# Hybrid decoder trunk, branch D: the triangular inverse's matmuls issued in turn over array positions, in one burst a step

## The chip, the cores and the metric

The kernel runs on one core of a Trainium2 chip. The metric is the device time of one execution in microseconds (us); the median of the runs shown counts. A profiled execution gives the trace; its rows are written as engine, line of the kernel, operation and tile. PE is TensorE, PEld its weight loads, DVE is VectorE, ACT is ScalarE, POOL is GpSimd and SP is SyncE, whose queue issues the transfers.

## The reference

One post-norm decoder layer over 256 tokens of width 1024: one wide input projection, five parallel branches with six heads of 64 (four heads of 96 in the last), gates, merging and a layer norm. The change touches branch D, a gated delta rule in chunks of 64 tokens:

```python
M = jnp.where(strict, jnp.einsum('bhnid,bhnjd->bhnij', kb, k) * decay, 0.0)
T = lax.linalg.triangular_solve(M + eye, ..., left_side=True, lower=True)
u = T @ (v * beta[..., None])
w = T @ (kb * jnp.exp(gc)[..., None])
...
def step(state, inp):
    v_new = u_i - w_i @ state
    o = qd_i @ state + qk_i @ v_new
    state = state * gl_i[..., None, None] + jnp.swapaxes(kd_i, -1, -2) @ v_new
```

So the inverse of a lower triangular matrix with ones on its diagonal is wanted for every head and chunk, and then a substitution over the chunks. The kernel sets up the whole 256-token triangle per head as two halves of 128 rows, inverts the diagonal blocks of 64, and substitutes block by block.

## The kernel before

**Units and ticks.** The weights stream in as units of up to 128x1024. For each unit the SP queue issues a load into one of seven `raw` buffers (L176), ScalarE makes the rounded high part `hi` (L123), VectorE the rest `lo` (L124), and TensorE multiplies in three passes, high by high, high by low, low by high (`mm3`, L128). A unit of a projection has three chunks, of 9, 9 and 6 matmuls; the chunk is followed by one tick. At each tick `stepper` advances up to three of the side streams by one `yield` each: the branches' own work is written as generators in the order base, c, levels, solve, b, a, gate_d, cross, norm. A plain `yield` makes a stream wait for the next tick, `yield 2` for the one after it. The program order of every engine comes from this interleaving; a planner in the framework then lays out each engine's queue, using its own model of the times, and may move an instruction ahead of others whose operands it takes to be late. Each engine works off its queue in order.

**Branch D.** The stream `base` (`d_base`) writes the 16x16 diagonal blocks of AT through a scratch in DRAM, inverts all of them on VectorE (L532, L534), writes the inverses to a second scratch (L542), and loads them with sixteen transfers (L550) into two tiles: Tc, the inverses, and Uc, their transposes. `levels` (`d_levels`) combines blocks of 16 to 32 and blocks of 32 to 64. Each such step is a product of a lower-left block with an inverse (`y`, L565 and L589), an evacuation to SBUF (L568, L593), a second product (`z`, L574 and L598; for the smaller size also its transpose `zt`, L576) and an evacuation on VectorE (L580, L582, L601). There are twelve blocks (six heads, two halves), and each position of 32 or 64 rows of the array handles twelve products in a row before the next position begins, with a tick in between. `solve` (`d_solve`) runs two generators of three heads side by side, each with matmuls (L617, L626, L632) and evacuations (L619, L628, L634) in turn. The PSUM tiles of all these steps come from a pool `tp` with two buffers. What follows is the output product (L648 to L651), a norm, the gate of branch D, and `mem_norm`, which waits for the flag `od` and makes the normalized memory that the last projections multiply.

An fp32 matmul of the program appears in the trace as two matmul records.

Of the kernel before, what the change touches and what calls it, by code (L numbers as in the profile page):

```python
# [12 lines left out]
ALU = mybir.AluOpType  # L13
AX = mybir.AxisListType

P = 128
# [4 lines left out]
H = 6  # L21
HD = 64
# [26 lines left out]
C_ID, C_TRI, C_ONE, C_LO, C_MA, C_MG1, C_MG2, C_MG3 = (  # L49
    0, 128, 256, 384, 385, 769, 1153, 1537)  # L50
# [25 lines left out]
def kernel(ctx: ExitStack, tc: tile.TileContext, T: dict, out: bass.AP):  # L76
# [7 lines left out]
    dr = ctx.enter_context(tc.tile_pool(name="dr", bufs=1, space=bass.MemoryType.DRAM))  # L84

    V_, A_, PE, G_ = nc.vector, nc.scalar, nc.tensor, nc.gpsimd
    uid = [0]

    def nm(s):
# [25 lines left out]
    def tpps(shape):  # L115
        return pst("tp", shape, 2)
# [6 lines left out]
        A_.activation(hi, src, AF.Copy)  # L123
        V_.tensor_tensor(lo, src, hi.bitcast(F32), op=ALU.subtract)  # L124

    def mm3(pt, lh, ll, rh, rl, first, last, keep=False):
        for l, r, start, stop in ((lh, rh, first, False), (lh, rl, False, False), (ll, rh, False, last)):
            ins = PE.matmul(pt, l, r, start=start, stop=stop)  # L128
            if keep:
                tc.keep_in_program_order(ins)  # L130

    def together(*products):
# [17 lines left out]
    def K(o, n=P):  # L150
        return cst[:, o:o + n]
# [96 lines left out]
    def stepper(gens, n, force=False):  # L248


        k = 0
        for g in list(gens):
            if k == n:
                break
            if not force and ready.get(id(g), 0) > tick[0]:
                continue
            try:
                d = next(g)
                if d is not False:
                    k += 1  # L260
                    ready[id(g)] = tick[0] + (GAP if d is None else d)
            except StopIteration:
                gens.remove(g)
# [244 lines left out]
    def d_base():  # L508

        yield from wait("AT")  # L510
        AT = R["AT"]
        ascr = dr.tile([8, 12, 16, 16], F32, name="ascr")
        t16, u16 = ct("t16", (96, 16, 16)), ct("u16", (96, 16, 16))
        a16, tmp = ct("a16", (96, 16, 16)), ct("tmp16", (96, 225))

        Tc, Uc = R["Tc"], R["Uc"] = spt("pr", (P, 12, 32), bufs=NPR), f3t(shape=(P, 12, 64))
        G_.memset(Tc, 0.0)
        G_.memset(Uc, 0.0)
        for b in range(8):
            r = slice(16 * b, 16 * b + 16)  # L520
            nc.sync.dma_start(ascr[b].rearrange("g j c -> j g c"), AT[r, 0:12, r])
            if b % 2:
                yield
        V_.memset(t16, 0.0)
        V_.memset(t16.rearrange("p i c -> p (i c)")[:, 0::17], 1.0)
        yield
        nc.sync.dma_start(a16, ascr.rearrange("b g j c -> (b g) j c"))
        for _ in range(4):
            yield
        for i in range(1, 16):  # L530
            pr = tmp[:, :i * i].rearrange("p (c j) -> p c j", c=i)
            V_.tensor_tensor(pr, t16[:, 0:i, 0:i].rearrange("p j c -> p c j"),  # L532
                             a16[:, 0:i, i][:, None, :].to_broadcast([96, i, i]), op=ALU.mult)
            V_.tensor_reduce(t16[:, i, 0:i], pr, axis=AX.X, op=ALU.add, negate=True)  # L534
            if i % 2 or i > 8:
                yield
        V_.tensor_copy(u16, t16.rearrange("p i c -> p c i"))
        yield
        scrs = []
        for src in (t16, u16):  # L540
            scr = dr.tile([8, 12, 16, 16], F32, name=nm("scr"))
            nc.sync.dma_start(scr.rearrange("b g j c -> (b g) j c"), src)  # L542
            scrs.append(scr)
        for _ in range(3):
            yield
        for b in range(8):
            r = slice(16 * b, 16 * b + 16)
            for scr, dst, n in zip(scrs, (Tc, Uc), (2, 4)):
                c = slice(16 * (b % n), 16 * (b % n) + 16)
                nc.sync.dma_start(dst[r, :, c], scr[b].rearrange("g j c -> j g c"))  # L550
            yield
        for _ in range(3):
            yield
        flag("base")

    def d_levels():

        yield from wait("base")
        AT, Tc, Uc = R["AT"], R["Tc"], R["Uc"]

        y = tpps((P, 12, 16))
        for b in range(4):
            r = slice(32 * b, 32 * b + 32)
            for g in range(12):
                PE.matmul(y[r, g], AT[r, g, r], Tc[r, g, 0:16], start=True, stop=True)  # L565
            yield
        ys = spt("Y", (P, 12, 32), bufs=1)
        A_.activation(ys[:, :, 0:16], y, AF.Copy)  # L568
        yield
        z, zt = tpps((P, 12, 16)), tpps((P, 12, 16))  # L570
        for b in range(4):
            r, c = slice(32 * b, 32 * b + 32), 32 * (b % 2)
            for g in range(12):
                PE.matmul(z[32 * b:32 * b + 16, g], ys[r, g, 0:16], Uc[r, g, c + 16:c + 32], start=True, stop=True)  # L574
                if b % 2 == 0:
                    PE.matmul(zt[r, g], Uc[r, g, 0:32], ys[r, g, 0:16], start=True, stop=True)  # L576
            yield
        for b in range(4):
            r, c = slice(32 * b, 32 * b + 32), 32 * (b % 2)
            V_.tensor_scalar(Uc[32 * b:32 * b + 16, :, c + 16:c + 32], z[32 * b:32 * b + 16], -1.0, None, op0=ALU.mult)  # L580
            if b % 2 == 0:
                V_.scalar_tensor_tensor(Tc[r, :, 0:16], zt[r], K(C_LO, 1)[r], Tc[r, :, 0:16], op0=ALU.mult, op1=ALU.add)  # L582
            yield

        ab = [(slice(64 * b, 64 * b + 32), slice(64 * b + 32, 64 * b + 64)) for b in range(2)]
        y = tpps((P, 12, 32))
        for i, j in ab:
            for g in range(12):
                PE.matmul(y[j, g], AT[i, g, j], Tc[i, g], start=True, stop=True)  # L589
            yield  # L590
        ys = spt("Y", (P, 12, 32), bufs=1)
        for i, j in ab:
            A_.activation(ys[j], y[j], AF.Copy)  # L593
        yield
        z = tpps((P, 12, 32))
        for i, j in ab:
            for g in range(12):
                PE.matmul(z[i, g], ys[j, g], Uc[j, g, 32:64], start=True, stop=True)  # L598
            yield
        for i, j in ab:  # L600
            V_.tensor_scalar(Uc[i, :, 32:64], z[i], -1.0, None, op0=ALU.mult)  # L601
        yield
        flag("levels")

    def d_solve():

        yield from wait("levels")
        AT, PT, Uc, V = R["AT"], R["PT"], R["Uc"], R["V"]
        W = f3t(shape=(P, 2, 6, HD))

        def solve(g):
            hs, hsl = range(3 * g, 3 * g + 3), slice(3 * g, 3 * g + 3)
            for t in range(2):
                if t == 1:
                    pt = tpps((P, 3, HD))
                    for x, h in enumerate(hs):
                        PE.matmul(pt[:, x], AT[:, 12 + h], W[:, 0, h], start=True, stop=True)  # L617
                    yield
                    V_.tensor_tensor(V[:, 1, hsl], V[:, 1, hsl], pt, op=ALU.subtract)  # L619
                    yield  # L620
                for b in range(2):
                    r = slice(64 * b, 64 * b + 64)
                    if b == 1:
                        pt = tpps((P, 3, HD))
                        for x, h in enumerate(hs):
                            PE.matmul(pt[r, x], AT[0:64, 6 * t + h, r], W[0:64, t, h], start=True, stop=True)  # L626
                        yield
                        V_.tensor_tensor(V[r, t, hsl], V[r, t, hsl], pt[r], op=ALU.subtract)  # L628
                        yield
                    pt = tpps((P, 3, HD))  # L630
                    for x, h in enumerate(hs):
                        PE.matmul(pt[r, x], Uc[r, 6 * t + h], V[r, t, h], start=True, stop=True)  # L632
                    yield
                    V_.tensor_copy(W[r, t, hsl], pt[r])  # L634
                    yield

        live = [solve(0), solve(1)]
        while live:
            stepper(live, 2)
            yield 1  # L640
        od = R["od"] = f3t(shape=(P, 2, 6, HD))
        rq = R["rq"]
        lg = lgps()[:, :, :384].rearrange("p t (h d) -> p t h d", h=6)
        for t in range(2):
            pt = lg[:, t]
# [335 lines left out]
    fin = {}  # L981
# [15 lines left out]
    def out_units():  # L997
# [3 lines left out]
        def out_mm(u, k, t, i, first, last):  # L1001
            lo, hi = PC[t][i]
            ts = slice(t * P, (t + 1) * P)
            yh, yl = (y[:, k % 3, ts] for y in yhl[k // 3])
            if k > 5:
                h, l = (x[lo // 512][:, lo % 512:lo % 512 + hi - lo] for x in (u.h, u.l))
            else:
                h, l = u.h[:, lo:hi], u.l[:, lo:hi]
            mm3(fin["p"][t][i][:, :hi - lo], yh, yl, h, l, first, last, keep=not first)

        def chunk(u, k, t):
            if k == 0 and t == 0:
# [169 lines left out]
```

## Time and profile before

| what | us |
|---|---|
| runs | 488.65, 488.16, 487.26; median 488.16 |
| the profiled execution | 489.4 |
| its span, first to last instruction | 487.6 |
| TensorE busy | 469.8, 96% of the span |
| VectorE busy | 336.1, 69% |
| ScalarE busy | 270.6, 55% |
| mean granted clock of TensorE | 0.977 of full speed |

Busy time of TensorE is the union of the modelled spans of its matmuls, which overlap; a busy TensorE is not one at its peak. The difference between the profiled execution's time and its span, 1.8 us, lies before the first and after the last instruction.

### The profile page before, as it was taken

How to read it: one execution, taken by the hardware profiler on the slowest of the kernel's cores; microseconds unless marked ns; L12 is line 12 of the kernel's file. 1: busy time of each engine (PE TensorE's matmuls, PEld its weight loads, DVE VectorE, ACT ScalarE, POOL GpSimd, SP SyncE). 2: the span in 40 equal slices, each digit the busy share in tenths (PEclk: the TensorE clock that was granted, in tenths of full speed). 3: DMA queues.
4: the chain of work that ended last, by engine and by line, in shares of the span. 5: the costliest groups of instructions: out<-in, count | busy, mean ns of one | idle time of the engine just before them, and what ended most of it. 6: DMA issues, size and time to landing. Idle time of an engine off the chain costs nothing.

```text
span 487.6 us, 10147 instructions
## 1 busy us (share of the span) xinstructions
PE 469.8 (96%) x3957; PEld 439.2 (90%) x3957; DVE 336.1 (69%) x764; ACT 270.6 (55%) x521; POOL 30.5 (6%) x36
## 2 busy tenths in 40 slices
PE   7999999989989999999999999999999999999994
PEld 3999999979988999999999999988987899999973
DVE  4898998875983435568976665666667457678747
ACT  5546684763773333466854455846657445566610
POOL 0000040120000000000001210000012111100000
PEclk9999999989998699999999999999999999999997
DMA  8995667554444113245656786252753345577302
GB/s 263 367 369 169 202 202 250 161 144 121 146 105 116 44 60 114 84 140 174 204 155 209 222 260 215 78 167 77 279 191 120 104 125 173 182 231 235 131 1 86
DMA packets 35050, 81.38 MB, mean 167 GB/s; under 512 B 8969, under 2 KB 17467, under 8 KB 34875
## 3 DMA queue, kind: packets, MB, share of 16 engines
q1 hardware_dynamic: 34715, 80.22, 52.1%
q8 instruction: 31, 0.51, 0.4%
q10 hardware_dynamic: 288, 0.52, 0.3%
q14 instruction: 16, 0.13, 0.1%
HBM read 79.37 MB, written 1.36 MB: 166 GB/s over the span
## 4 chain that ended last, share of the span: by engine, by line
PE 84%; DVE 6%; DMA 4%; ACT 3%; issue 1%; SPq 1%; POOL 0%; DVEq 0%; POOLq 0%
PE mm L128 67%; PE lg L135 3%; PE lg L128 2%; DVE lo L124 2%; PE tp L128 2%; ACT pr L754 2%; PE av L135 2%; PE lg L897 1%; PE lg L773 1%; DMA raw<-in_wcs_dram 1%; ACT hi L123 1%; DVE pr L738 1%; DMA scr<-t 1%; PE av L920 1%; PE tp L632 1%
## 5 line engine op out<-in xcount | busy, mean ns | idle before, releaser
L124 DVE TENSOR_TENSOR lo<-raw,hi 128x1024 fp32r<-128x1024 f32 (+4 forms) x163 | 170.7, 1049 | 89.6 <-ACT hi L123 89.0
L128 PE MATMUL mm<-xhi,hi 128*128 128x256 f32 x776 | 221.3, 285 | 0.4 <-ACT hi L123 0.4
L123 ACT ACTIVATE hi<-raw 128x1024 fp32r<-128x1024 f32 (+4 forms) x163 | 146.4, 901 | 131.8 <-PE mm L128 90.2
L128 PE MATMUL mm<-xhi,lo 128*128 128x256 f32 x776 | 219.2, 283 | 0.3 <-DVE lo L124 0.3
L128 PE MATMUL mm<-xlo,hi 128*128 128x256 f32 x776 | 219.0, 282 | 0.0
L128 PEld LDWEIGHTS mm<-xhi,hi 128*128 128x128 f32 x776 | 148.1, 191 | 3.9 <-issue 2.0
L128 PEld LDWEIGHTS mm<-xhi,lo 128*128 128x128 f32 x776 | 147.9, 191 | 3.4 <-issue 1.6
L128 PEld LDWEIGHTS mm<-xlo,hi 128*128 128x128 f32 x776 | 148.2, 191 | 0.9 <-issue 0.7
L128 PE MATMUL mm<-f,hi 128*128 128x256 f32 x240 | 45.3, 283 | 0.4 <-ACT hi L123 0.4
L972 POOL TENSOR_TENSOR yacc<-yacc,yt 128x256 f32<-128x256 f32 x24 | 19.8, 824 | 303.3 <-DVE yt L971 294.1
L128 PEld LDWEIGHTS mm<-f,hi 128*128 128x128 f32 x240 | 36.7, 188 | 0.9 <-ACT hi L123 0.6
L128 PE MATMUL mm<-f,lo 128*128 128x256 f32 x120 | 33.9, 283 | 0.0
L128 PEld LDWEIGHTS mm<-f,lo 128*128 128x128 f32 x120 | 22.6, 188 | 0.1
L754 ACT ACTIVATE pr<-pr,mm 128x128 f32<-128x128 f32 (+1 forms) x36 | 15.9, 444 | 4.8 <-DVE mm L745 4.8
L954 ACT ACTIVATE th<-mm,bcol 128x256 f32<-128x256 f32 x40 | 18.4, 460 | 0.0
L128 PE MATMUL mm<-hi,xhi 128*128 128x384 f32 (+1 forms) x48 | 15.8, 353 | 2.0 <-ACT hi L123 2.0
L128 PE MATMUL mm<-lo,xhi 128*128 128x384 f32 (+1 forms) x48 | 16.8, 349 | 0.4 <-DVE lo L124 0.4
L135 PE MATMUL lg<-f,f 64*128 64x256 f32 (+1 forms) x144 | 16.9, 351 | 0.0
L738 DVE CUSTOM_DVE_ANT_0 pr<-lg,cst 128x128 f32<-128x128 f32 (+1 forms) x48 | 14.4, 352 | 3.6 <-PE lg L135 3.6
L971 DVE SCALAR_TENSOR_TENSOR yt<-th,mm 128x256 f32<-128x256 f32 x32 | 13.5, 420 | 4.7 <-PE mm L128 2.9
L128 PE MATMUL mm<-hi,xlo 128*128 128x384 f32 (+1 forms) x48 | 16.5, 345 | 0.0
L480 POOL TENSOR_SCALAR_AFFINE_SELECT pr<-pr 128x256 f32<-128x256 f32 x6 | 9.5, 1591 | 93.9 <-DVE pr L479 93.9
(234 smaller groups left out, 570.6 us busy)
## 6 DMA issues: line engine op xcount, KB each, us to landing
raw<-in_wf_dram SPq DMA_DIRECT2D x60, 512.0 KB, 4.5
raw<-in_wm_dram SPq DMA_DIRECT2D x40, 512.0 KB, 3.6
raw<-in_wb_dram SPq DMA_DIRECT2D x40, 192.0 KB, 2.4
raw<-in_wt_dram SPq DMA_DIRECT2D x12, 384.0 KB, 3.6
raw<-in_wo_dram SPq DMA_DIRECT2D x8, 512.0 KB, 5.9
gr<-gscr SPq DMA_DIRECT2D x12, 128.0 KB, 3.6
raw<-in_wcs_dram SPq DMA_DIRECT2D x3, 402.0 KB, 6.3
raw<-in_mem_dram SPq DMA_DIRECT2D x2, 512.0 KB, 3.2
```

The source lines that it names most:

```text
L123: A_.activation(hi, src, AF.Copy)
L124: V_.tensor_tensor(lo, src, hi.bitcast(F32), op=ALU.subtract)
L128: ins = PE.matmul(pt, l, r, start=start, stop=stop)
L135: PE.matmul(pt, l, r, start=start, stop=stop)
L480: G_.affine_select(E[:, 0::2], E[:, 0::2], pattern=[[0, 2], [1, P]], compare_op=ALU.is_ge, fill=-BIG, base=0, channel_multiplier=-1)
L632: PE.matmul(pt[r, x], Uc[r, 6 * t + h], V[r, t, h], start=True, stop=True)
L738: V_.tensor_tensor_reduce(l[:, sl], pts[x][:, sl], mk[x][:, sl], 1.0, 3.0e38, ALU.add, ALU.min, mx[x][:, t, g:g + 1])
L754: A_.activation(l[:, sl], l[:, sl], AF.Exp, bias=mms[x][:, t:t + 1], scale=-1.0, accum_out=sm_[x][:, t, g:g + 1])
L773: PE.transpose(lg[:, x, i * P:(i + 1) * P], L[x][0][:, i * P:(i + 1) * P], ident)
L954: A_.activation(th, p, AF.Tanh, bias=bcol[:, i:i + 1], scale=0.5)
L971: V_.scalar_tensor_tensor(yt, st_["th"], 1.0, st_["p"], op0=ALU.add, op1=ALU.mult)
L972: (V_ if last else G_).tensor_tensor(yacc[:, d], yacc[:, d], yt, op=ALU.add)
```

## The change

Four things are edited. The flag that ends the base step is raised after twelve yields instead of three. In the levels, the loops are turned round: the outer loop runs over the twelve blocks and the inner one over the array positions, each step is issued within one tick, z and zt one behind the other, and `yield 2` stands where a result of another engine is used next; VectorE's evacuations are issued in one tick too, Tc's first. The substitution takes all six heads in one step, without the two generators. Each of these matmuls is pinned with `keep`, which orders it behind the TensorE instruction that the program gave before it. The argument `keep` of `mm3` is renamed to `pin`.

```diff
+    keep = tc.keep_in_program_order
...
-        for _ in range(3):
+        for _ in range(12):
             yield
         flag("base")
...
+        br = [(slice(32 * b, 32 * b + 32), 32 * (b % 2)) for b in range(4)]
         y = tpps((P, 12, 16))
-        for b in range(4):
-            r = slice(32 * b, 32 * b + 32)
-            for g in range(12):
-                PE.matmul(y[r, g], AT[r, g, r], Tc[r, g, 0:16], start=True, stop=True)
-            yield
+        for g in range(12):
+            for r, c in br:
+                keep(PE.matmul(y[r, g], AT[r, g, r], Tc[r, g, 0:16], start=True, stop=True))
+        yield
         ys = spt("Y", (P, 12, 32), bufs=1)
         A_.activation(ys[:, :, 0:16], y, AF.Copy)
-        yield
+        yield 2
         z, zt = tpps((P, 12, 16)), tpps((P, 12, 16))
...
+        for g in range(12):
+            for r, c in br:
+                keep(PE.matmul(z[r.start:r.start + 16, g], ys[r, g, 0:16], Uc[r, g, c + 16:c + 32], start=True, stop=True))
+        for g in range(12):
+            for r, c in br[0::2]:
+                keep(PE.matmul(zt[r, g], Uc[r, g, 0:32], ys[r, g, 0:16], start=True, stop=True))
+        yield
+        for r, c in br[0::2]:
+            V_.scalar_tensor_tensor(Tc[r, :, 0:16], zt[r], K(C_LO, 1)[r], Tc[r, :, 0:16], op0=ALU.mult, op1=ALU.add)
+        for r, c in br:
+            V_.tensor_scalar(Uc[r.start:r.start + 16, :, c + 16:c + 32], z[r.start:r.start + 16], -1.0, None, op0=ALU.mult)
+        yield 2
...
-        for i, j in ab:
-            for g in range(12):
-                PE.matmul(y[j, g], AT[i, g, j], Tc[i, g], start=True, stop=True)
-            yield
+        for g in range(12):
+            for i, j in ab:
+                keep(PE.matmul(y[j, g], AT[i, g, j], Tc[i, g], start=True, stop=True))
+        yield
...
-        yield
+        yield 2
         z = tpps((P, 12, 32))
...
+        for g in range(12):
+            for i, j in ab:
+                keep(PE.matmul(z[i, g], ys[j, g], Uc[j, g, 32:64], start=True, stop=True))
+        yield
...
+                pt = tpps((P, 6, HD))
+                for h in range(H):
+                    keep(PE.matmul(pt[r, h], Uc[r, 6 * t + h], V[r, t, h], start=True, stop=True))
+                yield
+                V_.tensor_copy(W[r, t], pt[r])
+                yield
-        live = [solve(0), solve(1)]
-        while live:
-            stepper(live, 2)
-            yield 1
```

## Rows read from the trace of the kernel before

**Rows 1.** The page, part 4: the chain that ended last, by engine.
```profile
PE 84%; DVE 6%; DMA 4%; ACT 3%; issue 1%; SPq 1%; POOL 0%; DVEq 0%; POOLq 0%
```
**Rows 2.** Windows: length, busy time of each engine, granted clock, DMA share, GB/s.
```profile
143.70:147.86 4.16, 1.91 (x50) 1.79 (x50) 0.85 (x1) 0.81 (x1) 0.00 (x0) 1.00 0.28 28
147.86:151.28 3.42, 3.42 (x17) 3.42 (x18) 1.22 (x1) 1.06 (x1) 0.00 (x0) 0.50 0.19 17
151.28:161.50 10.22, 10.22 (x175) 8.49 (x175) 5.05 (x19) 5.40 (x15) 0.00 (x0) 1.00 0.41 127
161.50:171.76 10.26, 10.26 (x106) 9.70 (x106) 3.69 (x8) 2.21 (x3) 0.00 (x0) 0.50 0.17 53
171.76:183.00 11.24, 11.24 (x161) 10.28 (x161) 3.18 (x5) 4.35 (x7) 0.00 (x0) 1.00 0.22 67
183.00:208.00 25.00, 25.00 (x237) 23.89 (x238) 12.99 (x25) 9.04 (x14) 0.00 (x0) 1.00 0.34 101
```
**Rows 3.** Groups of TensorE, 143.7 to 183 us: busy, mean ns; idle before, releaser.
```profile
L128 PE MATMUL mm<-xhi,hi 128*128 128x256 f32 x40 | 13.8, 345 | 0.0
...
L574 PE MATMUL tp<-f,Y 32*16 32x16 f32 x96 | 5.2, 178 | 0.0
L576 PE MATMUL tp<-Y,f 32*32 32x16 f32 x48 | 3.5, 193 | 0.0
L565 PE MATMUL tp<-pr,big 32*32 32x16 f32 x96 | 3.4, 178 | 2.3 <-DMA pr<-scr 2.3
L773 PE MATMUL lg<-cst,pr 128*128 128x128 f32 x13 | 3.1, 348 | 0.0
L135 PE MATMUL av<-pT,f 128*64 128x256 f32 (+1 forms) x24 | 2.6, 339 | 0.0
...
L135 PE MATMUL lg<-f,f 64*128 64x128 f32 (+1 forms) x8 | 0.9, 350 | 0.0
```
**Rows 4.** The chain in order of time: start, length, what, how many records.
```profile
147.80 3.85 PE mm L128 x18
151.65 0.66 PE lg L773 x6
152.30 0.80 PE av L135 x8
153.10 1.52 PE tp L565 x48
...
159.60 0.69 PE tp L574 x24
...
175.49 0.87 PE tp L589 x24
...
181.41 1.53 PE tp L598 x48
...
255.84 46.61 PE mm L128 x405
```
**Rows 5.** Windows of L565 alone, TensorE and weight loads: matmuls under way.
```profile
153.40:153.50 0.10, 0.10 (x9) 0.10 (x6) 1.00 1.17 123
153.70:153.80 0.10, 0.10 (x12) 0.10 (x10) 1.00 0.66 164
```
**Rows 6.** Last load of Tc in SP's queue; time to landing of L550's transfers.
```profile
151.01 0.44 SPq L550 DMA_DIRECT2D pr<-scr  x1
...
DMA to landing us min/median/max: 1.6/1.8/3.4
```
**Rows 7.** Groups of VectorE, 143.7 to 183 us.
```profile
L124 DVE TENSOR_TENSOR lo<-raw,hi 128x1024 fp32r<-128x1024 f32 x6 | 7.4, 1225 | 11.7 <-ACT hi L123 11.5 <-PE mm L128 0.2
...
L601 DVE TENSOR_SCALAR f<-tp 32x384 f32<-32x384 f32 x1 | 0.5, 546 | 1.1 <-PE tp L598 1.1
```
**Rows 8.** Products on the normalized memory: count, ns min/median/max, first and last start.
```profile
L128 PE MATMUL mm<-big,hi x48: 278/283/384, 321.5 to 333.8; 128*128 128x256 f32 x48
```
**Rows 9.** Timeline of TensorE: the first burst of the solve.
```profile
185.93 0.91 PE L632 MATMUL tp<-f,f 64*64 64x64 f32 x12
```

More of the change, by code (lines that the diff above doesn't have):

```diff
@@ L124, in split, with mm3 @@
         V_.tensor_tensor(lo, src, hi.bitcast(F32), op=ALU.subtract)
-    def mm3(pt, lh, ll, rh, rl, first, last, keep=False):
+    def mm3(pt, lh, ll, rh, rl, first, last, pin=False):
         for l, r, start, stop in ((lh, rh, first, False), (lh, rl, False, False), (ll, rh, False, last)):
             ins = PE.matmul(pt, l, r, start=start, stop=stop)
-            if keep:
+            if pin:
                 tc.keep_in_program_order(ins)
@@ L567, in d_levels @@
+        yield
         ys = spt("Y", (P, 12, 32), bufs=1)
         A_.activation(ys[:, :, 0:16], y, AF.Copy)
-        yield
-        z, zt = tpps((P, 12, 16)), tpps((P, 12, 16))
-        for b in range(4):
-            r, c = slice(32 * b, 32 * b + 32), 32 * (b % 2)
-            for g in range(12):
-                PE.matmul(z[32 * b:32 * b + 16, g], ys[r, g, 0:16], Uc[r, g, c + 16:c + 32], start=True, stop=True)
-                if b % 2 == 0:
-                    PE.matmul(zt[r, g], Uc[r, g, 0:32], ys[r, g, 0:16], start=True, stop=True)
-            yield
@@ L578, in d_levels @@
[L578 to L582, printed above, removed]
-            yield
+        yield 2
+        z, zt = tpps((P, 12, 16)), tpps((P, 12, 16))
+        for g in range(12):
+            for r, c in br:
+                keep(PE.matmul(z[r.start:r.start + 16, g], ys[r, g, 0:16], Uc[r, g, c + 16:c + 32], start=True, stop=True))
@@ L586, in d_levels @@
         y = tpps((P, 12, 32))
-        for i, j in ab:
-            for g in range(12):
-                PE.matmul(y[j, g], AT[i, g, j], Tc[i, g], start=True, stop=True)
-            yield
+        for g in range(12):
+            for i, j in ab:
+                keep(PE.matmul(y[j, g], AT[i, g, j], Tc[i, g], start=True, stop=True))
+        yield
         ys = spt("Y", (P, 12, 32), bufs=1)
@@ L593, in d_levels @@
             A_.activation(ys[j], y[j], AF.Copy)
-        yield
[L595 to L599, printed above, removed]
+        yield 2
+        z = tpps((P, 12, 32))
+        for g in range(12):
+            for i, j in ab:
+                keep(PE.matmul(z[i, g], ys[j, g], Uc[j, g, 32:64], start=True, stop=True))
+        yield
         for i, j in ab:
@@ L609, in d_solve @@
         W = f3t(shape=(P, 2, 6, HD))
[L611 to L617, printed above, removed]
+        for t in range(2):
+            if t == 1:
+                pt = tpps((P, 6, HD))
+                for h in range(H):
+                    keep(PE.matmul(pt[:, h], AT[:, 12 + h], W[:, 0, h], start=True, stop=True))
+                yield
+                V_.tensor_tensor(V[:, 1], V[:, 1], pt, op=ALU.subtract)
+                yield
+            for b in range(2):
+                r = slice(64 * b, 64 * b + 64)
+                if b == 1:
+                    pt = tpps((P, 6, HD))
+                    for h in range(H):
+                        keep(PE.matmul(pt[r, h], AT[0:64, 6 * t + h, r], W[0:64, t, h], start=True, stop=True))
@@ L618, in solve @@
                     yield
-                    V_.tensor_tensor(V[:, 1, hsl], V[:, 1, hsl], pt, op=ALU.subtract)
+                    V_.tensor_tensor(V[r, t], V[r, t], pt[r], op=ALU.subtract)
                     yield
[L621 to L635, printed above, removed]
@@ L637, in d_solve @@
-        live = [solve(0), solve(1)]
-        while live:
-            stepper(live, 2)
-            yield 1
+                pt = tpps((P, 6, HD))
+                for h in range(H):
+                    keep(PE.matmul(pt[r, h], Uc[r, 6 * t + h], V[r, t, h], start=True, stop=True))
+                yield
+                V_.tensor_copy(W[r, t], pt[r])
+                yield
         od = R["od"] = f3t(shape=(P, 2, 6, HD))
@@ L1008, in out_mm @@
                 h, l = u.h[:, lo:hi], u.l[:, lo:hi]
-            mm3(fin["p"][t][i][:, :hi - lo], yh, yl, h, l, first, last, keep=not first)
+            mm3(fin["p"][t][i][:, :hi - lo], yh, yl, h, l, first, last, pin=not first)
         def chunk(u, k, t):
```

## The prediction, on record before the result was known

> **What bounds the kernel now.** I read the page first: TensorE carries 84% of the chain that ended last [rows 1]. The order of TensorE's instructions is therefore the clock of the kernel, and an edit is worth what it takes out of that queue. Then I looked for the stretch where the edited lines run, and cut the time around them into windows by granted clock [rows 2]. They run from 143.7 to 183.0 us, 39.3 us in all. The reader should see three things there: a stretch of 4.16 us in which TensorE has only 1.91 us of work; then 3.42 us at clock 0.50; and, after a stretch at full clock that holds many small products, 10.26 us more at 0.50. VectorE and ScalarE are busy for 14 of the 39.3 us each, so they are not the limit here. Next came the groups of that stretch [rows 3] and the chain of work in order of time [rows 4] give counts and prices. Last I looked at where two array positions meet [rows 5], at the DMA queue that feeds the first step [rows 6], and at what hangs on the end of the branch [rows 7 to 9].
>
> **What fills the 39.3 us.** An fp32 product leaves two matmul records. Work that the change doesn't touch: 120 projection matmuls (three rows of 40 [rows 3]) at 46.61/405 = 115 ns [rows 4] are 13.8 us; 13 transposes of L773 at 0.66/6 = 110 ns, 1.4 us; 32 records of L135, four groups of eight at 0.80 us, 3.2 us. Together 18.4 us at full clock. The small products at full clock: L565, 96 at 1.52/48 = 31.7 ns, 3.0 us; L574, 96 at 0.69/24 = 28.8 ns, 2.8 us; L576, 48 with the same weights' shape as L565, at its price 1.5 us; L589, 48 at 0.87/24 = 36 ns, 1.7 us; L598, 48 at 1.53/48 = 31.9 ns, 1.5 us [rows 3, 4]. Together 10.5 us. The first step also stands idle for 2.3 us, waiting for the load of Tc [rows 3]. What is left, 39.3 - 18.4 - 10.5 - 2.3 = 8.1 us, is half clock and changes of shape. At half clock 18 projection matmuls took 3.85 us, 214 ns each instead of 115 [rows 4]; if all work in the 3.42 + 10.26 = 13.7 us stretched like that, it lost 13.7 x (1 - 115/214) = 6.3 us. That leaves 1.8 us for some 17 changes between kinds of matmul, about 0.1 us each.
>
> **Edit 1, the flag of the base step comes 12 yields after the last load instead of 3.** Today the first products reach TensorE at 144.9 and wait 2.3 us. Nine more ticks put nine more chunks of projection ahead of them. Chunks are 9, 9 and 6 products, 8 on average, so nine are 72 x 115 ns = 8.3 us, and the attention products of that stretch come on top. From 143.7 that is 152.0 at the earliest and about 155 with three groups of L135 and ten transposes (3.5 us). The last load of Tc leaves its queue at 151.01 and lands 1.8 us later as a median, 152.8, and 154.4 at the slowest [rows 6]. So the wait becomes between 0 and 2.4 us; I take 0, since the median lies ahead of 155. What fills the former gap are projections whose weights are already split: VectorE and ScalarE had less than 1 us of work in the idle 4.16 us, so they had run ahead. No load moves: the sixteen L550 transfers stay where they are in the queue. The ticks are given back: the levels go from 19 ticks to 11, so the solve begins one tick later in program order. One tick is about 1 us of other work, and what needs the branch's end next, the normalized memory, is first multiplied at 321.5 [rows 8], over 100 us away. Price nothing.
>
> **Edit 2, the positions take turns.** Per step the count of products is unchanged. The question is whether products at different positions run at once. In the burst of L565 where one position's twelve end and the next one's begin, a window of 0.10 us has 12 matmuls in flight, against 9 on either side [rows 5]; so two positions do overlap there, as long as both have work near the head of the queue. Ends: full overlap divides the 32-row steps over four positions and the zt and 64 steps over two: 24 x 31.7 + 24 x 28.8 + 24 x 31.7 + 24 x 36 + 24 x 31.9 ns = 3.85 us. Only pairs overlap: 1.52 + 1.38 + 0.76 + 0.87 + 0.77 = 5.3 us. No overlap: 10.5 us. I take 4.6, midway between pairs, which the row shows, and four. The steps also shrink from eleven bursts to four, so changes of shape fall from 17 to about 10: 1.1 us instead of 1.8.
>
> The Trainium skill ("TensorEngine Tiling (Array Packing)", Gotcha 1: PSUM Pressure) speaks against this: it says that different row tiles can't access the same PSUM bank at the same time, and here all positions of a step write one PSUM tile. The row disagrees: both positions of that seam write the same tile y. By the rule the bursts would keep 10.5 us and the sum would be 480.1. The skill also has a floor ("TensorE: Matmul & The Clock Gate", Wait — 56ns, not 53.3ns?): starts never closer than about 25 ns, however few columns. An estimate by it is 336 x 25 ns = 8.4 us for the bursts and 478.0 in all; 12 in flight against 9 in the same window says that two positions together beat it.
>
> **Edit 3, the clock.** The granted clock fell to 0.50 at 147.86, after the idle gap and the first two lone bursts, and at 161.50, after a stretch with three bursts of small products between projections [rows 2, 4]. With the gap filled and the bursts at 4.6 us in place of 10.5, TensorE's time in this stretch is mostly projections, as from 183 to 208 us, where bursts of 0.91 us [rows 9] stand between them and the clock stays 1.00 [rows 2]. So I expect no half clock here: 6.3 us come back. Bounds: all of it, or none.
>
> **Edit 4, six heads in one substitution step.** The three-head bursts already run back to back (one row of 12 records in 0.91 us; there are seven such bursts from 185.9 to 207.9 [rows 9]), at one position a step, so TensorE gains nothing. VectorE gets one operation for two. Its longest work in the queue is a split of 1.2 us [rows 7], and a step has over 3 us until the next burst. Nothing, on either side up to one switch of 0.1 us a step. The renamed argument in mm3 does nothing. Pinning fixes the order only against earlier products; projections are all ready, so it costs nothing where no operand is late; the price if one is late stands with the rivals.
>
> **Sum.** The stretch becomes 18.4 + 4.6 + 1.1 = 24.1 us instead of 39.3: 15.2 us less. Behind 183 us TensorE is busy nearly throughout, so an earlier end stays earlier. The profiled execution took 489.4 us (span 487.6 and 1.8 around it): 489.4 - 15.2 = 474.2. That execution is 1.2 us above the median of the runs, 488.16, so the median would be some 473; I say 474.
>
> **Rivals.**
> *Positions do not overlap beyond the seam.* Then the bursts stay 10.5: 489.4 - 9.3 = 480.1. For it: inside one position starts are 32 ns apart whatever the columns. Against: the 12 in flight.
> *The half clock stays.* The bursts of small products are still there, now denser in time. 6.3 us are not won: 480.5. For it: the second fall came after small products without any idle time. Against: bursts at 153.1 and after 183 at full clock.
> *Pinned bursts wait for VectorE or ScalarE* (the other side). Ten bursts (three in the levels, seven in the solve) need a result that another engine made one or two ticks before. Queued behind one of them on TensorE is everything else. A split of 1.2 us plus an evacuation of up to 0.55 us [rows 7] ahead of each would cost, if TensorE had no distance, 1.75 us; ten are 17.5 us, and the time would be 489.4 - 15.2 + 17.5 = 491.7. It decides against the change from 1.7 us a burst (17 us: 0.3% above). For it: the first step shows that the program order can run ahead of the operands. Against: the same spacing in the solve costs TensorE no wait today, with VectorE busy 13.0 of 25.0 us [rows 2].
> *A new order later on.* The planner lays out every engine's queue by its own times, and a shift may make a wait elsewhere: 478 to 488.
>
> **How the numbers follow.** What measurement can tell from no change is about 0.3%, 1.5 us. Forecast 0.62 (its own range 469 to 477, from 3.85 to 5.3 us of bursts, up to 2.4 us of wait and a few us of reordering); no overlap 0.09; half clock stays wholly or in part 0.15; waits of pinned bursts 0.05; new order 0.09. Faster by over 0.3%: the first three and most of the last, 0.90; the same 0.04; slower 0.06. The range is 467 to 483: below, full overlap and a kinder order; above, either of the two middle rivals with some waiting.
>
> **What would show it.** Edit 1: no idle time of TensorE before L565's successor, and no releaser from the load of Tc. Edit 2: matmuls at different positions a few ns apart, 96 in 0.8 to 1.5 us. Edit 3: granted clock 1.00 from 143 us to the solve. Edit 4: seven bursts of the solve as long as before, without a wait for VectorE. The solve begins about 15 us earlier than 185.9. The prediction is wrong if the bursts take 10 us, if the clock falls within them, or if that gain appears at the solve and is lost by the end.

## The result, and the profile after

The changed kernel took 475.65 us as the median of four runs (474.59 to 476.90), the kernel before 487.74 beside it. The ratio is 0.9754, 95% interval 0.9723 to 0.9785: about 12.1 us less, where 474.0 was forecast. The profiled execution took 476.9 us with a span of 475.0, against 489.4 and 487.6. Lines of the kernel have moved by up to four: mm3 is L130 now, y is L569 and L592, z L577 and L601, zt L580, the solve's product L633.

The page, chain by engine, answers to [rows 1]; TensorE's order sets the time still more plainly:

```profile
PE 89%; ACT 4%; DVE 2%; issue 1%; DMA 1%; POOL 1%; SPq 0%; DVEq 0%
```

The windows of the changed kernel from the end of the base step to the solve and beyond it, columns as in [rows 2]. No window is at 0.50, TensorE is busy all but 0.24 us of them, and 290 matmuls pass in 9.30 us:

```profile
143.35:154.70 11.35, 11.35 (x95) 9.89 (x93) 6.12 (x13) 6.43 (x12) 0.00 (x0) 1.00 0.30 39
154.70:164.00 9.30, 9.06 (x290) 8.02 (x289) 5.61 (x19) 5.86 (x15) 0.00 (x0) 1.00 0.70 259
164.00:175.58 11.58, 11.58 (x177) 10.95 (x176) 6.71 (x12) 5.52 (x9) 0.00 (x0) 1.00 0.23 67
175.58:198.00 22.42, 22.42 (x212) 21.56 (x212) 11.23 (x18) 7.13 (x12) 0.00 (x0) 1.00 0.34 106
```

TensorE's groups from 143.35 us to the solve, as in [rows 3]. The 2.3 us of waiting for the load are gone from y, and 174 projection matmuls (three rows of 58) fit in where there were 120:

```profile
L130 PE MATMUL mm<-xlo,hi 128*128 128x256 f32 x58 | 16.6, 287 | 0.0
...
L769 PE MATMUL lg<-cst,pr 128*128 128x128 f32 x15 | 2.8, 280 | 0.0
...
L577 PE MATMUL tp<-f,Y 32*16 32x16 f32 x96 | 1.5, 175 | 0.2 <-issue 0.2
...
L601 PE MATMUL tp<-f,Y 32*32 32x32 f32 x48 | 1.2, 192 | 0.0
L580 PE MATMUL tp<-Y,f 32*32 32x16 f32 x48 | 1.1, 179 | 0.0
L569 PE MATMUL tp<-pr,big 32*32 32x16 f32 x96 | 1.0, 180 | 0.0
L592 PE MATMUL tp<-pr,big 32*32 32x32 f32 x48 | 0.9, 192 | 0.0
```

The chain in order of time, as in [rows 4]. Each burst's share of the queue stands in it: y 0.92 us, where its 96 records took over 3 before; the second size 0.88 and 0.17 + 0.87; and the solve's first burst is unchanged (0.91 us in the timeline) and begins there at 175.58 instead of 185.93 ([rows 9]; the chain has it from 175.65). That is 10.35 us earlier, with more projections ahead of it than before:

```profile
154.83 0.92 PE tp L569 x70
...
159.95 0.14 PE tp L577 x2
...
160.35 0.15 PE tp L577 x4
...
160.86 0.67 PE tp L577 x54
161.53 0.24 issue
161.76 0.32 PE tp L577 x20
162.08 0.37 PE tp L580 x17
...
163.25 0.55 PE tp L580 x28
...
167.30 0.88 PE tp L592 x48
...
171.12 0.17 PE tp L601 x2
...
171.72 0.87 PE tp L601 x46
...
175.65 0.84 PE tp L633 x12
```

Windows of y alone, as in [rows 5]: by the modelled ends, 34 matmuls are under way in a tenth of a microsecond, where one position had 9 and the seam 12.

```profile
155.00:155.10 0.10, 0.10 (x34) 0.10 (x24) 1.00 0.51 205
155.30:155.40 0.10, 0.10 (x34) 0.10 (x25) 1.00 0.69 287
```

SP's queue, as in [rows 6]: the last load of Tc leaves at 152.07 and by the median lands 1.9 us later, 154.0; y starts at 154.76.

```profile
152.07 0.44 SPq L552 DMA_DIRECT2D pr<-scr  x1
...
DMA to landing us min/median/max: 1.6/1.9/3.4
```

The products on the normalized memory, as in [rows 8], begin at 308.9 instead of 321.5. That is 12.6 us earlier, the same as the difference of the spans: nothing is given back behind the branch.

```profile
L130 PE MATMUL mm<-big,hi x48: 278/283/384, 308.9 to 321.3; 128*128 128x256 f32 x48
```

### The profile page after: what moved, and what is told of

The parts are those of the page before. It is cut to its first block, busy times and chain, and to the rows that moved or that the text cites. A ratio compares the mean times of both kernels' runs of the same rounds, so it can differ in the third digit from the quotient of the medians.

```text
span 475.0 us, 10138 instructions
## 1 busy us (share of the span) xinstructions
PE 458.2 (96%) x3957; PEld 428.5 (90%) x3957; DVE 334.2 (70%) x757; ACT 269.7 (57%) x521; POOL 31.4 (7%) x36
## 4 chain that ended last, share of the span: by engine, by line
PE 89%; ACT 4%; DVE 2%; issue 1%; DMA 1%; POOL 1%; SPq 0%; DVEq 0%
PE mm L130 71%; PE lg L137 4%; PE lg L130 2%; ACT pr L750 2%; PE tp L130 2%; ACT hi L125 2%; PE lg L893 2%; DMA raw<-in_wcs_dram 1%; PE av L137 1%; PE lg L769 1%; PE av L916 1%; PE tp L633 1%; POOL pr L482 1%; DVE lo L126 0%; DVE pr L753 0%
## 5 line engine op out<-in xcount | busy, mean ns | idle before, releaser
L130 PE MATMUL mm<-xhi,hi 128*128 128x256 f32 x776 | 218.7, 282 | 0.5 <-ACT hi L125 0.4
L130 PE MATMUL mm<-xhi,lo 128*128 128x256 f32 x776 | 217.4, 281 | 0.3 <-DVE lo L126 0.3
L130 PE MATMUL mm<-xlo,hi 128*128 128x256 f32 x776 | 216.8, 279 | 0.0
L130 PEld LDWEIGHTS mm<-xhi,hi 128*128 128x128 f32 x776 | 146.1, 188 | 3.7 <-issue 1.7
L130 PEld LDWEIGHTS mm<-xhi,lo 128*128 128x128 f32 x776 | 145.8, 188 | 3.6 <-issue 1.9
L130 PEld LDWEIGHTS mm<-xlo,hi 128*128 128x128 f32 x776 | 146.2, 188 | 0.9 <-issue 0.7
L130 PE MATMUL mm<-f,hi 128*128 128x256 f32 x240 | 45.5, 284 | 0.3 <-ACT hi L125 0.3
L130 PEld LDWEIGHTS mm<-f,hi 128*128 128x128 f32 x240 | 36.8, 188 | 0.9 <-ACT hi L125 0.5
L130 PE MATMUL mm<-f,lo 128*128 128x256 f32 x120 | 33.9, 282 | 0.0
L130 PEld LDWEIGHTS mm<-f,lo 128*128 128x128 f32 x120 | 22.6, 188 | 0.0
L130 PE MATMUL mm<-hi,xhi 128*128 128x384 f32 (+1 forms) x48 | 16.2, 361 | 3.2 <-ACT hi L125 3.2
L130 PE MATMUL mm<-lo,xhi 128*128 128x384 f32 (+1 forms) x48 | 17.6, 366 | 0.4 <-DVE lo L126 0.4
L130 PE MATMUL mm<-hi,xlo 128*128 128x384 f32 (+1 forms) x48 | 17.2, 358 | 0.0
L967 DVE SCALAR_TENSOR_TENSOR yt<-th,mm 128x256 f32<-128x256 f32 x32 | 13.4, 420 | 4.5 <-PE mm L130 2.7
```

What stands on the lines that cost most here:

```text
L967: V_.scalar_tensor_tensor(yt, st_["th"], 1.0, st_["p"], op0=ALU.add, op1=ALU.mult)
```

## The experiments

Each is timed against the kernel before, whose median was 487.02 us beside the first four and 487.08 beside the last four.

### Positions one after the other again

All edits stay; within a burst the two loops are exchanged, at all five places like this:

```diff
-        for g in range(12):
-            for r, c in br:
+        for r, c in br:
+            for g in range(12):
                 keep(PE.matmul(y[r, g], ...
```

> All edits kept, pinned and one burst a step, but inside a burst the twelve products of one array position come before those of the next. Theory (products at different positions run at once, and that is 5.8 us of the gain): the five groups of small products take some 10.8 us again instead of 5.0, so about 481.4 us, with the load wait still gone; if the longer bursts pull the clock down too, up to 486. Rival (turn-taking gives nothing beyond a seam; gap and clock are the whole gain): 475.7 us, within 1 us.

481.82 us, ratio 0.9898 (0.9863 to 0.9932). More than half of the gain is gone, so the rival falls. The timeline of TensorE and the windows of this kernel (columns as in [rows 2]):

```profile
152.33 2.91 PE L569 MATMUL tp<-pr,big 32*32 32x16 f32 x96
```
```profile
152.40:155.70 3.30, 3.30 (x101) 3.27 (x101) 3.14 (x14) 3.30 (x11) 0.00 (x0) 0.99 1.02 392
155.70:159.10 3.40, 3.40 (x18) 3.40 (x18) 0.59 (x3) 0.05 (x1) 0.00 (x0) 0.50 0.42 143
159.10:165.90 6.80, 6.80 (x162) 5.97 (x162) 1.73 (x3) 2.46 (x4) 0.00 (x0) 1.00 0.26 80
165.90:169.30 3.40, 3.40 (x28) 3.36 (x26) 2.50 (x7) 0.19 (x1) 0.00 (x0) 0.50 0.00 0
```

The same 96 records take 2.91 us instead of 0.99. In the chain of this kernel the five groups hold 10.0 us, 5.0 in the changed one. The clock falls half a microsecond behind the long burst of y and again with that of z and zt, although TensorE is never idle here. So taking turns brings 5.0 us by itself, and between these two profiled executions the half clock in the levels goes with it.

### The flag after three yields

```diff
-        for _ in range(12):
+        for _ in range(3):
             yield
         flag("base")
```

> The changed kernel with the base flag after 3 yields again. Theory (the nine extra ticks take the wait for Tc away): the pinned burst of all four positions stands at TensorE's head some 10 us earlier in program order, before the last load of Tc lands at about 154, so TensorE waits up to 9 us there, and the clock falls behind the gap: 482 to 489 us. Rival (the planner places the burst late anyway, the flag does nothing): 475.7 us, no wait for the load.

480.94 us, ratio 0.9853 (0.9808 to 0.9898). The flag matters, but the wait of 9 us that I expected isn't there: TensorE waits 0.6 us for the load of Tc, because other products stand between the pieces of the burst (the chain holds it in five pieces from 142.82 to 151.43). That the planner took part of it as not ready fits, but isn't shown. The loss stands elsewhere, in a gap of 2.6 us in the middle of the zt burst, and in the clock, which falls within that gap. What the gap is comes in the last section. Timeline and windows of this kernel:

```profile
155.10 0.46 PE L580 MATMUL tp<-Y,f 32*32 32x16 f32 x18
158.16 1.03 PE L580 MATMUL tp<-Y,f 32*32 32x16 f32 x30 [2.60 <-issue]
```
```profile
154.20:156.80 2.60, 1.36 (x115) 1.22 (x114) 1.18 (x5) 1.51 (x4) 0.00 (x0) 1.00 0.46 181
156.80:163.60 6.80, 5.44 (x51) 5.41 (x52) 3.38 (x7) 1.18 (x2) 0.00 (x0) 0.50 0.01 2
```

### Only the flag

The same line as above in the kernel before, 3 to 12, and nothing else.

> The kernel before with only the flag after 12 yields. Theory (gap and low-column bursts each cost clock of their own): the 2.3 us of wait and the first half-clock stretch (1.6 us) go, the second stretch behind the scattered bursts stays: about 483.8 us. Rival (all half clock follows from the idle gap): both stretches go, 479.5 us. Second rival (later levels delay what follows): 488 us or more.

485.66 us, ratio 0.9982 (0.9946 to 1.0019): not told apart from no change. Both expectations missed. In its profiled execution (483.22 us, clock 0.996) TensorE waits for no load and no window at 0.50 lies in the levels, as the rival said; yet it is 3.7 us above the rival's 479.5. Its ten runs go from 482.92 us at a mean clock of 0.996 to 488.77 at 0.981 and 488.75 at 0.978: in other executions the mean clock is lower, and the time follows it. Where it fell in those isn't recorded. Taking the wait away, without the other edits, is not enough to see a gain.

### The substitution of before

The two generators of three heads, unpinned, in place of the six-head steps; the rest as changed.

> The changed kernel with the substitution of before (two generators of three heads, not pinned). Theory (six heads a step give TensorE nothing): 475.7 us, within 0.8. Rival (fewer bursts and fewer VectorE operations bring part of the gain): 476.7 us or more.

475.47 us, ratio 0.9761 (0.9727 to 0.9795): the same as the change. Edit 4 is worth nothing that can be measured.

This kernel and the one with only the flag have the same flag and the same substitution; the levels alone differ, by edit 2 with its pins and yields. Neither profiled execution has half clock while TensorE works; both pages show the same row of the granted clock, in tenths, over 40 equal slices of the span, and TensorE's work ends ahead of the last slice's fall:

```profile
PEclk9999999999999999999999999999999999999998
```

They took 483.22 and 475.37 us. So edit 2 is worth 7.9 us where the clock has no part in it; the five groups of small products hold 11.0 and 5.0 us of the two chains. Between the medians, 485.66 and 475.47, it is 10.2.

### No pins

```diff
-    keep = tc.keep_in_program_order
+    keep = lambda ins: ins
```

> The changed kernel without the pins on its bursts. Theory (the bursts' order comes from program order; the pins only hold it): turn-taking and the load wait's absence stay, 475.7 us within 1.5. Rival (without the pins the planner moves the first burst ahead of the last load of Tc, or lets projections into the bursts): a wait for the load comes back, 478 to 483 us.

474.28 us, ratio 0.9748 (0.9719 to 0.9777), with the interval of the change. The burst of y stays whole:

```profile
153.84 0.99 PE L569 MATMUL tp<-pr,big 32*32 32x16 f32 x96
```

The order of the loops does the work, not the pins; and pins that could have made TensorE wait cost nothing that can be measured either.

### The flag after twenty yields

Twenty in place of twelve.

> The changed kernel with the base flag after 20 yields instead of 12, so the whole rest of branch D comes eight ticks later in program order. Theory (nothing waits for the end of the branch, and the load has landed at 12 already): 475.5 us within 1. Rival (the ticks are on the path): about eight ticks of 0.9 us, 483 us.

475.42 us, ratio 0.9761 (0.9728 to 0.9794). Eight ticks more cost nothing that can be measured: the end of the branch is not on the path.

### Half bursts, and z apart from zt

```diff
                 keep(PE.matmul(y[r, g], ...
-        yield
+            if g % 6 == 5:
+                yield
```

at all five products, and in a second kernel only one `yield` between z and zt.

> The changed kernel with each of the five groups of small products cut into two halves of six blocks, a tick of projections between them. Theory (a burst starts at 7 ns a matmul and falls to 15 ns, with gaps inside z and zt, because TensorE takes its instructions faster than they come; short bursts stay in the quick part): five more changes of shape at 0.1 us against some 1.5 us of slow part, 474.5 us. Rival (the slow part is the array's own): the changes cost 0.5 us and nothing comes back, 476.2 us.

> The changed kernel with one tick between z and zt, so that the longest run of small products, 144 matmul records, becomes 96 and 48. Theory (as for the half bursts, only the gap of 0.2 to 0.4 us inside this run goes): 475.2 us. Rival (nothing to gain): 475.7 us.

476.39 us, ratio 0.9792 (0.9765 to 0.9820), and 475.95 us, ratio 0.9787 (0.9761 to 0.9814). Nothing came back, so the theory of a slow second half fell. y in halves, in the timeline of the first of the two:

```profile
152.53 0.59 PE L569 MATMUL tp<-pr,big 32*32 32x16 f32 x48
154.30 0.59 PE L569 MATMUL tp<-pr,big 32*32 32x16 f32 x48
```

Two halves are 1.18 us, the whole 0.99: a half pays for its own first and last product (0.18 us each) and is no faster within.

## Why the prediction was right, and by how much

**The sum.** From 143.35 us to the solve the changed kernel needs 32.2 us, but holds 54 more projection matmuls than the 39.3 us of before; at 115 ns they are 6.2 us, so like for like it is 26.0, against 24.1 forecast. The stretch saves 13.3 us instead of 15.2. The sign that the solve would begin about 15 us earlier didn't come: it begins 10.35 us earlier, since it stands 29 projection matmuls (3.3 us) later in TensorE's order, more than the one tick that was forecast.

**Edit 1, the wait: as forecast.** The 2.3 us are gone, and y starts at 154.76, where about 155 was forecast, 0.8 us after the median landing, so it is near the edge, as the bounds said. That the flag takes the wait away is shown by the run with only the flag, where TensorE waits for no load. With the turned loops, three yields bring back 0.6 us of it, not the 9 I had named; what that run lost besides is another gap. What the prediction didn't have: alone the edit gives nothing that can be measured.

**Edit 2, turns: overlap as forecast, 5.5 us for 5.9 in the bursts.** The bursts hold 5.0 us of the chain (0.92, 1.28, 0.92, 0.88 and 1.04) where 4.6 was taken and 10.5 was there. Overlap over four positions is nearly full in y: 96 records take 0.99 us, 0.18 of it the last one's own length, so starts lie 8.5 ns apart; with one position in turn it is 28.8 ns (2.91 us in the run with exchanged loops), with two, as in L592, 16 ns. So "midway between pairs and four" was too careful for y (0.92 in the chain, between 0.76 and 1.52) and too hopeful for z (1.28, between 0.69 and 1.38), which is cut up by other matmuls; zt and L601 took 0.92 and 1.04 where 0.76 and 0.77 were priced. The exchange of the loops isolates the bursts' part, 10.0 against 5.0 us. The whole of edit 2 is more: 7.9 us at full clock, between the flag's kernel and that with the old substitution, where the forecast had 5.9 and 0.7 for fewer changes of shape.

The Trainium skill's rule against it ("TensorEngine Tiling (Array Packing)", Gotcha 1: PSUM Pressure) doesn't hold here: four positions write one PSUM tile with 34 matmuls under way. The Trainium skill's packing model ("TensorE: Matmul & The Clock Gate", Part 3: Packing small matmuls) puts 4 ns between starts at different positions; 8.5 ns is what this burst shows. The estimate of 8.4 us for the bursts, from starts 25 ns apart, falls by the same number.

**Edit 3, the clock: right in kind, too large.** In the profiled execution there is no half clock from 143 us to the solve. Clock and changes of shape together were 8.1 us; what is left unexplained in the new stretch is 32.2 - 20.0 (174 projections) - 1.7 (15 transposes) - 3.7 (attention products in the chain) - 5.0 - 0.2 = 1.6 us, so 6.5 came back where 7.0 was forecast (6.3 of clock and 0.7 of changes of shape). The remaining loss against the forecast is that the attention products took 3.7 us instead of 3.2 and two more transposes fell into the stretch. Together 2.3 (wait) - 0.2 (the new gap in z) + 5.5 + 6.5 - 0.7 = 13.4. Outside the stretch the two executions differ by where else the clock was low: before had 0.50 from 106.9 to 110.3 us, after from 11.6 to 15.1. Those windows are not the change's work, and cost some 0.4 us in balance; another 0.6 us is a later first matmul.

But 6.5 is a remainder, not the clock measured. The 6.3 took all work at half clock as stretched, and the chain of the kernel before has a group of z inside the window at 0.50 that isn't; at full clock, 24 of the same records took 0.69 us too [rows 4]:

```profile
166.30 0.69 PE tp L574 x22
```

The runs also share the gain out otherwise than the sum does. The profiled execution of the flag's kernel has neither the wait nor half clock, and is 6.2 us below that of before (483.22 against 489.4), where the forecast's prices make 10.2: 2.3 of wait, 6.3 of clock, and 1.6 for the window from 106.9 at the same price. Edit 2 then adds 7.9 where 6.6 was forecast. Some of the 4 us stands in the chain of the flag's kernel, where the small products hold 11.0 us for 10.5 and the attention products 3.7 for 3.2; the rest is not settled. So the sum came nearer than its terms did, which is in part luck.

This term was priced from one profiled execution, and the clock differs between executions. Runs of before, timed beside the first experiments, go from 484.25 us at a mean clock of 0.993 to 489.60 at 0.977, and the priced one lies at that end; the changed kernel's four go from 474.59 (0.997) to 476.90 (0.994), with one at 0.991 (475.94). The medians, 487.02 and 475.65, stand 2.8 and 1.1 us above the lowest times, so roughly 1.7 us of the gain in a typical execution are clock; sixteen runs against four make that uncertain. The lowest times stand 9.7 us apart. Half clock came in a gap (the run with three yields) and behind long bursts at one position (the exchanged loops, never idle), each in one profiled execution; which of them weighs more in the kernel before is not settled.

**Edit 4 and the pins: nothing that can be measured, as forecast.** Shown by the runs with the old substitution and without pins. The rival on the other side, pinned bursts that wait for VectorE, has no sign in the trace: TensorE waits for no evacuation.

**Moved ticks: nothing, as forecast.** Shown by the run with twenty yields.

## What to carry to other kernels

Small matmuls at different array positions run at once if the program issues them in turn: turn the loops so that the position is the innermost one. Over four positions the 96 records of y took a third of the time; the five groups together took half. Price a clock term from several executions, not from the profiled one alone, since the fall of the clock differs from run to run, and check it with two runs that differ in one edit and agree in clock. Before pinning an order or splitting a burst, look whether the order is already kept; here neither moved the time.

## What the runs showed of the hardware that was not expected

Three things. In the profiled executions the clock fell behind bursts of 2.9 us at one position at a time while TensorE had no idle time, and did not fall behind the same products in 0.99 us. On average, starts over four positions are 8.5 ns apart in y and don't slow over 96 records. And a burst can stop with nothing in the profile to wait for: 2.6 us within 48 equal matmuls in the run with three yields. In that gap the DMA queues moved little but one packet of instructions; this is the row of that gap (queue, kind: packets, MB, share):

```profile
q8 instruction: 1, 0.02, 2.3%
```

The gap of 0.24 us in the changed kernel is the same kind of stop. Windows from the start of the span up to either stop, in the run with three yields and in the changed kernel, hold the same number of TensorE's records, 1370 or 1371 matmuls and as many weight loads, though the burst there is zt in one and z in the other:

```profile
0.00:155.56 155.56, 150.12 (x1370) 137.51 (x1370) 126.47 (x354) 96.69 (x188) 10.65 (x12) 1.00 0.65 208
```
```profile
0.00:161.53 161.53, 155.07 (x1371) 142.26 (x1371) 128.88 (x356) 98.45 (x192) 10.69 (x12) 0.99 0.63 202
```

So the place in TensorE's order counts, not the matmul. The queue of that packet, over the whole changed kernel:

```profile
q8 instruction: 31, 0.51, 0.4%
```

That is one packet of 16 KB for every 255 of TensorE's 7914 records. In the run with twenty yields the packet at that place starts at 162.27, when TensorE has done 1233 matmuls, and no stop of this size follows. In the other two TensorE is that far at 151.4 and 155.4 us, but the packet starts only at 155.90 and 159.48: in between, other transfers, mostly weights, held the DMA engines (89.8% of their time from 151.3 to 155.9 in the one, 98.9% from 155.3 to 159.5 in the other). It takes 0.96 and 0.94 us, and TensorE goes on 1.30 and 1.34 us after its end. So the traces say that TensorE ran out of instructions, which a burst of y uses up over ten times faster than projections do (8.5 against 115 ns a matmul); no run changes the arrival of that packet alone. Cutting z from zt went without the gap of 0.24 us and didn't move the time.
